# Two of the four weight sums of a 2x2 block product: accumulating transfers from the GpSimd queue in the place of VectorE additions

## The chip, the cores and the metric

The kernel runs on one core of one Trainium2 chip. The metric is the device time of one execution in microseconds (us). The time before is the median of three runs. About 0.3% (some 6 us here) is what a measurement of this kernel can tell from no change.

## The reference

Two transformer blocks run one after the other on 512 tokens of width 1024, all in float32. Only the parts around the change are shown; the attention and recurrence of both blocks are left out.

```python
def hybrid_layer(h, pos, ...):
    ...
    f = rmsnorm(h, norm_ff_w)
    return h + jnp.square(jax.nn.relu(f @ w_ff1)) @ w_ff2      # 1024 -> 4096 -> 1024

def swiglu(u, w_gate, w_up, w_down):
    return (jax.nn.silu(u @ w_gate) * (u @ w_up)) @ w_down     # 1024 -> 2816 -> 1024

def second_block(x, c, ...):
    ...
    u = modulate(rmsnorm_2(h, g_ff1[l]), sh1, sc1)
    h = h + FFN_RES * gt1[:, None, :] * swiglu(u, w1_gate[l], w1_up[l], w1_down[l])
    ...                                                        # attention, mLSTM, merge
    u = modulate(rmsnorm_2(h, g_ff2[l]), sh3, sc3)
    h = h + FFN_RES * gt3[:, None, :] * swiglu(u, w2_gate[l], w2_up[l], w2_down[l])
```

So there are three feed-forward layers: one in the first block (called FF here) and two in the second (FFN1 and FFN2).

## The kernel before

Every float32 product is made from three reduced-precision matmuls. Each operand is split into a rounded high part and the remainder: `split` (L113) lets ScalarE (ACT) write the high part (`wh`, L116) and VectorE (DVE) subtract it from the source (`wl`, L117). TensorE (PE) then multiplies low by high, high by low and high by high.

The first layer of each feed-forward is worked in groups. A group (`w_group`) multiplies a 2x2 block matrix of weights, A11, A21, A22 and A12 (`src[0]` to `src[3]`, each a 128x1024 tile of 512 KB), with a 2x2 block matrix of activations. It does so with seven block products instead of eight, in the manner of Winograd. `w_prod` issues one such product, 24 matmuls of 128x256 (L493). The price of leaving out the eighth product is additions. Those on the weights are four per group, on DVE:

- S = A11 + A21 (L530), into a tile `wS` of its own, of which there is one buffer
- A21 = A21 + A22 (L538), in place
- A11 = A11 + A21 (L539), in place, from the new A21; its split feeds the third product
- A12 = A12 + A11 (L549), in place

There are 8 groups in FF (numbered 0 to 7), 9 in FFN1 (8 to 16) and 9 in FFN2 (17 to 25), 26 in all. In FF the products are finished by multiplications with a row of scales `R` (L305) before they are split as `hh`, `hl`; in FFN1 and FFN2 by a product of two halves (L636).

The order of the products on PE is A11 (first), S, A11', A22, A12, A21', and the last with A12'. The first product of the next group follows the last of this one, so a steady group in the trace begins with 48 matmuls on the bank `x`.

Between the products `fill(j)` puts tiles of the down projection (the second layer), 12 matmuls of 128x512 each (L129 to L131), whose results take turns in two PSUM banks (`mm`). DVE empties such a bank into the residual `res` (L291 in FF, L616 in FFN1 and FFN2). A third tile cannot begin before the first has been emptied. The bank `x` of the products is emptied by L553 (`wq`), before the next product into it.

`w_load` (L473) loads one weight tile, called `raw` whatever its block, through the queue of SyncE (SP). A tile scheduler sets the order in which each engine takes its instructions; each engine then works in this order, and an instruction that waits holds up all that stands behind it on its engine. DVE also does a running product for the conditioning vector (L350).

Of the kernel before, what the change touches and what calls it, by code (L numbers as in the profile page):

```python
# [8 lines left out]
F32 = mybir.dt.float32  # L9
# [5 lines left out]
ALU = mybir.AluOpType  # L15
# [3 lines left out]
P = 128  # L19
T = 512  # L20
# [34 lines left out]
class Kern:  # L55
# [414 lines left out]
        small = self.raws if tag == "raw" else 2  # L470
        return (self.hp if own else self.wp).tile([P, KT, P], dt, name=tag, tag=("s_" if own else "") + tag, bufs=small if own else 3)

    def w_load(self, src, late=2):  # L473

        raw = self.w_tile("raw", F32, late < self.raws - 1).rearrange("p k m -> p (k m)")
        raw = raw[:, :src.shape[-1]]
        self.nc.sync.dma_start(out=raw, in_=src)
        return raw

    def w_split(self, raw, own):  # L480
# [23 lines left out]
    def w_group(self, src, u, tt, ready, evict, fill, early=False):  # L504


        nc, V, act, wk = self.nc, self.nc.vector, self.nc.scalar.activation, self.wk
        blk = lambda h, c: tuple((lambda k, t=t: t[:, 2 * k + h, c * HT:(c + 1) * HT]) for t in u)
        sums = lambda i: tuple((lambda k, t=t: t[:, k, i]) for t in tt)
        X, W, Z = self.bank("x"), self.bank("w"), self.bank("z")  # L510
        tmp = lambda n, tag, pool=wk, b=2: pool.tile([P, T], F32, name=n, tag=tag, bufs=b)
        A11, A21 = self.w_load(src[0], 0), self.w_load(src[1], 1)
        w = self.w_split(A11, True)
        self.w_prod(X, w, *blk(0, 0), first=True)
        p = tmp("wp_", "e1")
        act(out=p, in_=X, func=AF.Copy)
        fill(0)

        def z(A12):
            w = self.w_split(A12, True)  # L520
            self.w_prod(Z, w, *blk(1, 0), first=True)
            V.tensor_tensor(out=p, in0=Z, in1=p, op=ALU.add)

        A22 = A12 = None
        if early:
            A12 = self.w_load(src[3], 0)
            z(A12)
        ready()
        S = self.hp.tile([P, 2 * T], F32, name="wS", tag="wS", bufs=1)
        V.tensor_tensor(out=S, in0=A11, in1=A21, op=ALU.add)  # L530
        w = self.w_split(S, False)
        A22 = self.w_load(src[2])
        A12 = A12 if early else self.w_load(src[3], 0)
        self.w_prod(W, w, *sums(1), first=True)
        q = tmp("wq_", "e2")
        act(out=q, in_=W, func=AF.Copy)
        fill(1)
        V.tensor_tensor(out=A21, in0=A21, in1=A22, op=ALU.add)  # L538
        V.tensor_tensor(out=A11, in0=A11, in1=A21, op=ALU.add)  # L539
        w = self.w_split(A11, True)  # L540
        self.w_prod(X, w, *sums(2))
        un = tmp("wu_", "wu", self.hp, 1)
        act(out=un, in_=X, func=AF.Copy)
        w = self.w_split(A22, False)
        self.w_prod(W, w, *sums(3))
        V.tensor_tensor(out=un, in0=W, in1=un, op=ALU.subtract)
        if not early:
            z(A12)
        V.tensor_tensor(out=A12, in0=A12, in1=A11, op=ALU.add)  # L549
        evict(0, p, un)  # L550
        w = self.w_split(A21, True)
        self.w_prod(X, w, *sums(0))
        V.tensor_tensor(out=q, in0=q, in1=X, op=ALU.subtract)  # L553
        fill(2)
        w = self.w_split(A12, False)
        self.w_prod(X, w, *blk(1, 1))
        evict(1, X, q)
        fill(3)
# [638 lines left out]
    def attention1(self, ap):  # L1197
# [202 lines left out]
        V.tensor_scalar(out=wn05, in0=self.vec("gla_norm_w", 1), scalar1=0.5, scalar2=None, op0=ALU.mult)  # L1400
        go = lambda c, e, S: self.gla_out(c, a2, e, gv, S)
        gate = lambda *cc: self.gla_gate(cc, gv, sr, wn05)
        S = self.gla_meta(ap, a2, dmat, gh, gl, mA, gvm)

# [15 lines left out]

        e, so, S = {}, {}, [S]
        for step in PLAN.split():
# [9 lines left out]
            elif f == "g":  # L1432
                S.append(go(c, e[c], S[-1]))
            elif f == "s":
# [401 lines left out]
```

## Time and profile before

| | before |
|---|---|
| median of 3 runs | 1943.99 us (1940.88 to 1945.86) |
| the profiled execution | 1941.36 us, span 1939.6 us |
| PE busy | 1896.3 us, 98% of the span |
| DVE busy | 1491.1 us, 77% |
| ACT busy | 866.5 us, 45% |
| GpSimd (POOL) busy | 29.9 us, 2% |
| read from HBM | 225.74 MB, 121 GB/s over the span |
| mean granted clock of PE | 0.996 of full speed |

Busy time says how long an engine had work, the span how long the profiled execution took on the chip. The time of the execution has 1.8 us around the span. PE is the engine with nearly no idle time, so only what makes PE wait, or stop waiting, moves the end. The stretches of the trace that the groups fill are about 254 to 590 us (FF), 623 to 960 us (FFN1) and 1560 to 1900 us (FFN2).

### The profile page before, as it was taken

What the parts mean: (1) busy time and instruction counts of PE and PEld (TensorE: products, weight loads), DVE (VectorE), ACT (ScalarE), POOL (GpSimd) and SP (SyncE); (2) the same over time, 40 slices, a digit from 0 to 9 for tenths busy, and PEclk for the clock granted to TensorE, in tenths of its full rate; (3) what the DMA queues carried; (4) which work ended last, traced back from release to release, by engine and by line L of the source; (5) the groups of instructions that cost most, each with busy time, mean ns of one, the idle gap of its engine ahead of it and who ended that gap; (6) DMA issues with size and microseconds to landing.
All of it is one profiled execution on the core that took longest, in us unless ns stands there. A gap on an engine that the chain in (4) does not pass through costs nothing.

```text
span 1939.6 us, 27715 instructions
## 1 busy us (share of the span) xinstructions
PE 1896.3 (98%) x10808; PEld 1583.5 (82%) x10808; DVE 1491.1 (77%) x2592; ACT 866.5 (45%) x1406; POOL 29.9 (2%) x47
## 2 busy tenths in 40 slices
PE   8999999999999899999999999999999999999997
PEld 5775589999988599999887777776678888999996
DVE  6687599888888989888877745677758778877776
ACT  4334465443445544444455444344442245444443
POOL 0000000000000000000000000111100000000000
PEclk9999999999999999999999999999999999999998
DMA  6220145454534154555342231433348732333231
GB/s 197 67 61 12 47 167 167 141 154 147 169 97 146 60 174 146 170 159 179 120 142 87 87 119 58 110 92 96 89 163 298 262 121 78 119 110 109 89 97 55
DMA packets 74333, 240.48 MB, mean 124 GB/s; under 512 B 8997, under 2 KB 12214, under 8 KB 74202
## 3 DMA queue, kind: packets, MB, share of 16 engines
q1 hardware_dynamic: 57274, 189.75, 31.3%
q10 hardware_dynamic: 16928, 48.96, 8.0%
q8 instruction: 85, 1.39, 0.3%
q14 instruction: 46, 0.38, 0.1%
HBM read 225.74 MB, written 8.41 MB: 121 GB/s over the span
## 4 chain that ended last, share of the span: by engine, by line
PE 90%; DVE 7%; ACT 2%; DMA 1%; issue 1%; DVEq 0%; SPq 0%; ACTq 0%
PE x L493 14%; PE mm L131 11%; PE mm L130 11%; PE mm L129 11%; PE mm L123 6%; PE w L493 6%; PE mm L125 6%; PE mm L124 6%; PE z L493 3%; PE po L1652 1%; DVE wl L117 1%; PE sw L1624 1%; PE sc L1041 1%; PE pn L1049 1%; PE po L1178 1%
## 5 line engine op out<-in xcount | busy, mean ns | idle before, releaser
L116 ACT ACTIVATE wh<-raw 128x1024 fp32r<-128x1024 f32 (+1 forms) x371 | 386.3, 1044 | 434.3 <-PE mm L131 128.5
L117 DVE TENSOR_TENSOR wl<-raw,wh 128x1024 fp32r<-128x1024 f32 (+1 forms) x371 | 446.0, 1206 | 117.2 <-ACT wh L116 116.3
L131 PE MATMUL mm<-hh,wh 128*128 128x512 f32 (+1 forms) x640 | 244.7, 382 | 0.0
L130 PE MATMUL mm<-hl,wh 128*128 128x512 f32 (+1 forms) x640 | 244.0, 381 | 0.2 <-DVE hl L117 0.2
L129 PE MATMUL mm<-hh,wl 128*128 128x512 f32 (+1 forms) x640 | 241.6, 378 | 1.4 <-DVE res L688 1.3
L123 PE MATMUL mm<-uh,wl 128*128 128x512 f32 x560 | 224.9, 403 | 2.1 <-ACT uh L116 1.9
L125 PE MATMUL mm<-uh,wh 128*128 128x512 f32 x560 | 223.9, 400 | 0.0
L124 PE MATMUL mm<-ul,wh 128*128 128x512 f32 x560 | 222.9, 398 | 0.3 <-DVE ul L117 0.3
L130 PEld LDWEIGHTS mm<-hl,wh 128*128 128x128 f32 x640 | 120.2, 188 | 23.4 <-DVE hl L117 0.7
L129 PEld LDWEIGHTS mm<-hh,wl 128*128 128x128 f32 x640 | 120.1, 188 | 23.5 <-DVE res L688 1.5
L131 PEld LDWEIGHTS mm<-hh,wh 128*128 128x128 f32 x640 | 120.3, 188 | 21.6
L123 PEld LDWEIGHTS mm<-uh,wl 128*128 128x128 f32 x560 | 105.5, 189 | 35.0 <-issue 6.6
L124 PEld LDWEIGHTS mm<-ul,wh 128*128 128x128 f32 x560 | 105.6, 189 | 23.3 <-issue 1.5
L125 PEld LDWEIGHTS mm<-uh,wh 128*128 128x128 f32 x560 | 105.7, 189 | 23.1 <-issue 2.3
L493 PE MATMUL x<-vh,wl 128*128 128x256 f32 x416 | 116.2, 279 | 0.5 <-DVE wq__6195 L553 0.3
L493 PE MATMUL x<-uh,wl 128*128 128x256 f32 x416 | 115.3, 277 | 1.0 <-DVE wl L117 1.0
L493 PE MATMUL x<-vl,wh 128*128 128x256 f32 x416 | 115.5, 278 | 0.0
L493 PE MATMUL x<-vh,wh 128*128 128x256 f32 x416 | 115.1, 277 | 0.0
L493 PE MATMUL x<-ul,wh 128*128 128x256 f32 x416 | 115.0, 276 | 0.0
L493 PE MATMUL x<-uh,wh 128*128 128x256 f32 x416 | 115.0, 276 | 0.0
L350 DVE CUSTOM_DVE_ANT_0 adaw<-adaw,cb,c_vecs 128x1024 f32<-128x1024 f32 x72 | 91.4, 1278 | 15.0 <-DMA adaw<-in_w_ada 15.0
L616 DVE SCALAR_TENSOR_TENSOR res<-mm,gt,res 128x512 f32<-128x512 f32 x88 | 65.5, 747 | 23.3 <-PE mm L131 23.1
(960 smaller groups left out, 4250.3 us busy)
## 6 DMA issues: line engine op xcount, KB each, us to landing
adaw<-in_w_ada ACTq DMA_DIRECT2D x72, 512.0 KB
raw<-in_wgw SPq DMA_DIRECT2D x72, 512.0 KB
raw<-in_wdw SPq DMA_DIRECT2D x40, 512.0 KB
raw<-in_w_ffw SPq DMA_DIRECT2D x32, 512.0 KB
raw<-in_w_ffd SPq DMA_DIRECT2D x32, 512.0 KB
raw<-in_wgu SPq DMA_DIRECT2D x24, 512.0 KB
raw<-in_w_g SPq DMA_DIRECT2D x20, 512.0 KB
raw<-in_w_out SPq DMA_DIRECT2D x16, 512.0 KB
```

Source lines behind the costliest of these rows:

```text
L116: nc.scalar.activation(out=h, in_=src, func=AF.Copy)
L117: nc.vector.tensor_tensor(out=l, in0=src, in1=h.bitcast(F32), op=ALU.subtract)
L123: mm(ps, lhsT=wl[:, k], rhs=xh[:, k], start=(k == order[0]), stop=False)
L124: mm(ps, lhsT=wh[:, k], rhs=xl[:, k], start=False, stop=False)
L125: mm(ps, lhsT=wh[:, k], rhs=xh[:, k], start=False, stop=(k == order[-1]))
L129: mm(ps, lhsT=al, rhs=bh, start=(k == 0), stop=False)
L130: mm(ps, lhsT=ah, rhs=bl, start=False, stop=False)
L131: mm(ps, lhsT=ah, rhs=bh, start=False, stop=(k == last))
L350: ins = nc.vector.tensor_tensor_reduce(out=w, in0=w, in1=self.cb, scale=0.5, scalar=self.vec("b_ada_2", 72)[:, i:i + 1], op0=ALU.mult, op1 ...
L493: mm(o, lhsT=l[:, a, k], rhs=r(k), start=(first and a == 0 and k == 0 and j == 0), stop=(k == 3 and j == 2), skip_group_check=True)
L616: V.scalar_tensor_tensor(out=res[:, m], in0=ps, scalar=gt[:, m:m + 1], in1=res[:, m], op0=ALU.mult, op1=ALU.add)
L1041: mm(pk[:, :n], lhsT=k[:, kt, j * P:(j + 1) * P], rhs=q[:, kt, j * P:], start=(kt == 0), stop=(kt == 1))
```

## The change

S is no longer added on DVE: a second load through SP puts A11 into the tile `wS`, and a transfer from POOL's queue adds A21 to it on its way in. The load of A21 is likewise followed by a transfer from POOL's queue that adds A22 to it. A22 is still loaded by itself for its own product. L530 and L538 are gone, and the numbers of later lines rise: A11 = A11 + A21 is L543, A12 = A12 + A11 is L553, the emptying of `x` L557, that of `mm` in FFN1 and FFN2 L620, the products of two halves L640.

```diff
-    def w_load(self, src, late=2):
+    def w_load(self, src, late=2, plus=None):
 
         raw = self.w_tile("raw", F32, late < self.raws - 1).rearrange("p k m -> p (k m)")
         raw = raw[:, :src.shape[-1]]
         self.nc.sync.dma_start(out=raw, in_=src)
+        if plus is not None:
+
+            self.nc.gpsimd.dma_start(out=raw, in_=plus, accum_op=ALU.add)
         return raw
...
-        A11, A21 = self.w_load(src[0], 0), self.w_load(src[1], 1)
+        A11 = self.w_load(src[0], 0)
+        S = self.hp.tile([P, 2 * T], F32, name="wS", tag="wS", bufs=1)
+        nc.sync.dma_start(out=S, in_=src[0])
+        nc.gpsimd.dma_start(out=S, in_=src[1], accum_op=ALU.add)
+        A21 = self.w_load(src[1], 1, src[2])
...
         ready()
-        S = self.hp.tile([P, 2 * T], F32, name="wS", tag="wS", bufs=1)
-        V.tensor_tensor(out=S, in0=A11, in1=A21, op=ALU.add)
         w = self.w_split(S, False)
...
-        V.tensor_tensor(out=A21, in0=A21, in1=A22, op=ALU.add)
         V.tensor_tensor(out=A11, in0=A11, in1=A21, op=ALU.add)
```

The scheduler moves what remains. In the first place, group 2 of FF on DVE, the rows before are these; `raw_3047` is A11, `raw_3049` A21, `raw_3090` A22, and `mm_2920`, `mm_2940` and `mm_2954` are three tiles of the down projection one after the other:

```order
L553 TENSOR_TENSOR wq__2733<-wq__2733,x_2659 128x512 [waits PE_49]
L350 ISA adaw_3081,mods_2368<-adaw_3081,cb_2369,c_vecs_72 128x1024 [waits DMAHW6_49]
L350 ISA mods_2368 128x1
L117 TENSOR_TENSOR hl_2658<-wp__2694,hh_2657 128x2x256 [waits DVE_49,Activation_49]
L291 TENSOR_TENSOR res_2083<-mm_2920,res_2083 128x512 [waits PE_49]
L305 SCALAR_TENSOR_TENSOR wq__2733<-wq__2733,R_2398 128x512 [waits DVE_49]
L117 TENSOR_TENSOR wl_3011<-raw_3008,wh_3010 128x1024 [waits DMAHW3_49,Activation_49]
L291 TENSOR_TENSOR res_2083<-mm_2940,res_2083 128x512 [waits PE_49]
L530 TENSOR_TENSOR wS_3084<-raw_3047,raw_3049 128x1024 [waits DMAHW0_49]
L117 TENSOR_TENSOR hl_2658<-wq__2733,hh_2657 128x2x256 [waits DVE_49,Activation_49]
L538 TENSOR_TENSOR raw_3049<-raw_3049,raw_3090 128x1024 [waits DMAHW4_49,DVE_49]
L291 TENSOR_TENSOR res_2083<-mm_2954,res_2083 128x512 [waits PE_49]
```

Now the same place reads as follows; `raw_3049` is A11 here, `raw_3054` the A21 that two transfers fill, `mm_2922` the first of the three tiles:

```order
L350 ISA adaw_3087,mods_2368<-adaw_3087,cb_2369,c_vecs_72 128x1024 [waits DMAHW2_49]
L350 ISA mods_2368 128x1
L117 TENSOR_TENSOR hl_2659<-wp__2699,hh_2658 128x2x256 [waits DVE_49,Activation_49]
L117 TENSOR_TENSOR hl_2659<-wu__2824,hh_2658 128x2x256
L557 TENSOR_TENSOR wq__2736<-wq__2736,x_2660 128x512 [waits PE_49]
L543 TENSOR_TENSOR raw_3049<-raw_3049,raw_3054 128x1024 [waits DMASW5_49,DVE_49]
L291 TENSOR_TENSOR res_2083<-mm_2922,res_2083 128x512 [waits PE_49]
L305 SCALAR_TENSOR_TENSOR wq__2736<-wq__2736,R_2398 128x512 [waits DVE_49]
L117 TENSOR_TENSOR wl_3013<-raw_3010,wh_3012 128x1024 [waits DMAHW6_49,Activation_49]
L291 TENSOR_TENSOR res_2083<-mm_2942,res_2083 128x512 [waits PE_49]
```

A11 = A11 + A21 has moved up, from behind the fourth emptying of a bank to a place ahead of the first; its wait on `DMASW5` is the wait for POOL's accumulating transfer.

In the second place, a steady group of FFN2 on DVE, the rows before are these; `raw_16238` is A11, `raw_16240` A21 and `x_15935` the bank that the group's seventh product needs emptied:

```order
L538 TENSOR_TENSOR raw_16240<-raw_16240,raw_16278 128x1024 [waits DMAHW0_49,DVE_49]
L117 TENSOR_TENSOR wl_16275<-wS_16272,wh_16274 128x1024 [waits Activation_49]
L522 TENSOR_TENSOR wp__15970<-z_15937,wp__15970 128x512 [waits PE_49]
L117 TENSOR_TENSOR wl_16243<-raw_16238,wh_16242 128x1024 [waits Activation_49]
L636 TENSOR_TENSOR wp__15970<-wp__15970,wu__16072 128x512 [waits Activation_49]
L553 TENSOR_TENSOR wq__16006<-wq__16006,x_15935 128x512 [waits PE_49]
L539 TENSOR_TENSOR raw_16238<-raw_16238,raw_16240 128x1024 [waits DVE_49]
L117 TENSOR_TENSOR hl_15934<-wp__15970,hh_15933 128x2x256 [waits Activation_49]
L616 SCALAR_TENSOR_TENSOR res2_14027<-mm_16172,gt2_14559,res2_14027 128x512 [waits PE_49]
```

Now the same place reads as follows, with `raw_16260` for A11 and `raw_16265` for A21:

```order
L117 TENSOR_TENSOR wl_16299<-wS_16262,wh_16298 128x1024 [waits DMASW4_49,Activation_49]
L529 TENSOR_TENSOR wp__15995<-z_15958,wp__15995 128x512 [waits PE_49]
L117 TENSOR_TENSOR wl_16269<-raw_16260,wh_16268 128x1024 [waits DMAHW1_49,Activation_49]
L640 TENSOR_TENSOR wp__15995<-wp__15995,wu__16094 128x512 [waits Activation_49]
L543 TENSOR_TENSOR raw_16260<-raw_16260,raw_16265 128x1024 [waits DMASW5_49,DVE_49]
L117 TENSOR_TENSOR hl_15955<-wp__15995,hh_15954 128x2x256 [waits Activation_49]
L557 TENSOR_TENSOR wq__16029<-wq__16029,x_15956 128x512 [waits PE_49]
L117 TENSOR_TENSOR wl_16368<-raw_16260,wh_16367 128x1024 [waits Activation_49]
L620 SCALAR_TENSOR_TENSOR res2_14044<-mm_16194,gt2_14576,res2_14044 128x512 [waits PE_49]
```

The addition, with its wait for POOL's transfer, stands ahead of the emptying of `x` instead of behind it.

In the third place, the head of FFN1 on DVE, the addition and the split behind it now stand in the middle of a row of tiny instructions that works out a reciprocal square root for the layer's activations. Before, the same root (L186 and what follows) held none of them; L530 and the split of A11 stood in the root ahead of it:

```order
L186 TENSOR_SCALAR rs_v_5643<-s2_5634 128x4 [waits DVE_49]
L187 TENSOR_SCALAR rs_t_5644<-rs_v_5643 128x4 [waits DVE_49]
L188 TENSOR_SCALAR r2_5642<-rs_t_5644 128x4 [waits DVE_49]
L190 TENSOR_TENSOR rs_t_5644<-r2_5642 128x4 [waits DVE_49]
L191 SCALAR_TENSOR_TENSOR rs_t_5644<-rs_t_5644,rs_v_5643 128x4 [waits DVE_49]
```

Now the root begins as follows, with `raw_6135` for A11 and `raw_6140` for A21:

```order
L186 TENSOR_SCALAR rs_v_5651<-s2_5642 128x4 [waits DVE_49]
L543 TENSOR_TENSOR raw_6135<-raw_6135,raw_6140 128x1024 [waits DMASW1_49]
L187 TENSOR_SCALAR rs_t_5652<-rs_v_5651 128x4 [waits DVE_49]
L117 TENSOR_TENSOR wl_5873<-raw_5871,wh_5872 128x1024 [waits DMAHW6_49,Activation_49]
L188 TENSOR_SCALAR r2_5650<-rs_t_5652 128x4 [waits DVE_49]
L117 TENSOR_TENSOR wl_6212<-raw_6135,wh_6211 128x1024 [waits Activation_49]
L190 TENSOR_TENSOR rs_t_5652<-r2_5650 128x4 [waits DVE_49]
```

L543 and the split `wl_6212` stood some 80 instructions later before.

## Rows read from the trace of the kernel before

**Rows 1.** The page, busy time, share of the span and instructions of each engine

```profile
PE 1896.3 (98%) x10808; PEld 1583.5 (82%) x10808; DVE 1491.1 (77%) x2592; ACT 866.5 (45%) x1406; POOL 29.9 (2%) x47
```

**Rows 2.** Windows: stretch, length; busy PE, PEld, DVE, ACT, POOL; clock, DMA share, GB/s

```profile
254.00:320.00 66.00, 64.72 (x400) 57.05 (x399) 64.26 (x96) 37.06 (x51) 0.00 (x0) 1.00 0.42 133
320.00:590.00 270.00, 270.00 (x1739) 244.08 (x1738) 224.62 (x301) 116.47 (x145) 0.00 (x0) 1.00 0.48 145
615.00:620.00 5.00, 5.00 (x25) 4.02 (x23) 4.67 (x7) 4.21 (x7) 0.00 (x0) 1.00 1.01 362
650.00:670.00 20.00, 13.10 (x47) 9.33 (x48) 19.81 (x34) 11.05 (x18) 0.00 (x0) 0.91 0.05 14
700.00:710.00 10.00, 9.54 (x80) 9.11 (x79) 10.00 (x13) 5.39 (x9) 0.00 (x0) 1.00 0.49 151
720.00:960.00 240.00, 240.00 (x1726) 221.72 (x1725) 208.30 (x271) 106.80 (x132) 0.00 (x0) 1.00 0.50 158
1650.00:1660.00 10.00, 8.81 (x76) 8.51 (x75) 8.28 (x10) 4.23 (x6) 0.00 (x0) 1.00 0.34 111
1680.00:1900.00 220.00, 220.00 (x1582) 205.45 (x1581) 164.82 (x178) 97.61 (x119) 0.00 (x0) 1.00 0.32 97
```

**Rows 3.** Line L530: its instructions (shortest, median, longest ns), then its engine's wait

```profile
L530 DVE TENSOR_TENSOR wS<-raw x26: 1211/1222/1227, 260.8 to 1858.5; 128x1024 f32<-128x1024 f32 x26
...
  DMA raw<-in_wgw: 8.8, 11
```

**Rows 4.** Line L538: its instructions

```profile
L538 DVE TENSOR_TENSOR raw<-raw x26: 1215/1216/1226, 262.8 to 1860.3; 128x1024 f32<-128x1024 f32 x26
```

**Rows 5.** Chain that ended last, at two group starts: start us, length us, what

```profile
693.63 4.73 DMA raw<-in_wgw
...
1649.53 3.89 DMA raw<-in_wgw
...
1653.52 1.24 DVE wS L530
```

**Rows 6.** SP's queue: issue of A21's load, groups 2, 3, FFN1, FFN2

```profile
324.13 0.33 SPq L477 DMA_DIRECT2D raw<-in_w_ffw  x1
...
363.36 0.33 SPq L477 DMA_DIRECT2D raw<-in_w_ffw  x1
...
780.63 0.33 SPq L477 DMA_DIRECT2D raw<-in_wgw  x1
...
1764.67 0.33 SPq L477 DMA_DIRECT2D raw<-in_wgw  x1
```

**Rows 7.** DVE in order of time: start, length, line, operation, out<-in [idle before]

```profile
331.11 0.68 DVE L291 TENSOR_TENSOR res<-mm,res 128x512 f32<-128x512 f32 x1
...
371.03 0.68 DVE L553 TENSOR_TENSOR wq__3118<-wq__3118,x 128x512 f32<-128x512 f32 x1
...
623.33 1.22 DVE L530 TENSOR_TENSOR wS<-raw 128x1024 f32<-128x1024 f32 x1
...
628.60 0.17 DVE L186 TENSOR_SCALAR rs_v<-s 128x4 f32<-128x4 f32 x1
...
788.72 0.68 DVE L553 TENSOR_TENSOR wq__7082<-wq__7082,x 128x512 f32<-128x512 f32 x1
...
1768.44 1.23 DVE L530 TENSOR_TENSOR wS<-raw 128x1024 f32<-128x1024 f32 x1 [0.64 <-DMA raw<-in_wgw]
...
1774.79 0.68 DVE L553 TENSOR_TENSOR wq__16006<-wq__16006,x 128x512 f32<-128x512 f32 x1
```

**Rows 8.** Chain on PE: first matmul of two third tiles, seventh products of two groups

```profile
333.11 0.23 PE mm L129
...
374.14 0.23 PE mm L129
...
793.86 2.72 PE x L493 x24
...
1778.62 5.44 PE x L493 x48
```

## The prediction

> **What bounds the kernel now.** I read the page's busy times first. PE works 1896.3 us, 98% of the span, DVE 77%, POOL 2% [rows 1]. PE is the engine with hardly any idle time, so a DVE addition is worth something only where PE waits for DVE. The windows show where that is, and they were read next. In the long stretches of steady groups PE is busy for the whole of the stretch: 270.00 of 270 us in FF, 240.00 of 240 in FFN1, 220.00 of 220 in FFN2, while DVE has 224.62, 208.30 and 164.82 us of work there [rows 2]. Nothing can be gained in these 730 us. Idle time of PE near the groups stands in four places: 1.28 us at the start of FF (254 to 320, where DVE has 64.26 of 66), 6.90 us in the head of FFN1 (650 to 670, where DVE has 19.81 of 20), 0.46 us at 700 to 710 and 1.19 us at 1650 to 1660 [rows 2]. Their sum, 9.8 us, is all that the change could ever touch.
>
> Then I read the two lines that go. L530 has 26 instructions of 1.222 us, L538 26 of 1.216 us [rows 3, 4]: 63.4 us of DVE work leave. L530 stood behind a load 11 times, 8.8 us in all [rows 3]. The chain of waits runs through such a load at two group starts, from 693.63 and from 1649.53, and through L530 itself at 1653.52 [rows 5].
>
> **The change part by part.** I work each part as a difference and add it to the median of the runs, 1943.99; the profiled execution (1941.36, of which 1939.6 is span) lies 2.6 us below that median, and the durations are its own.
>
> *What goes.* In steady groups the 63.4 us are hidden behind a PE that is never idle: 0. At the start of group 18 the chain runs load 3.89, then L530 1.24, to the next product [rows 5]; S now comes ready-made, and the idle 1.19 us go. At 700 to 710 DVE is full for all of 10 us with L530 in it [rows 2]; the 0.46 us go. Together -1.7.
>
> *What is added.* 26 more loads through SP and 52 accumulating transfers through POOL, 512 KB each. That is 41 MB (78 x 524,288 bytes), of which 27 MB are accumulated. The DMA share in the steady stretches is 0.32 to 0.50 [rows 2], so there is room for it. S is read early (its load and transfer have most of a group's 30 us), and its split waits for nothing that is late: 0.
>
> The term that decides is A21. Before, A11 = A11 + A21 (L539) stood behind two DVE additions and needed only plain loads. Now, as L543, it waits for a chain: load of A21, then POOL wakes, then the accumulating transfer. While it waits, all of DVE stands, since the queue is in order. Let X be the time from A21's landing to the release of L543. No POOL transfer stands in this trace, so X is bounded by rows. A plain load takes 3.77 us from its issue (1764.67) to the DVE instruction that waited for it (1768.44) [rows 6, 7]. The accumulation reads two streams and writes one, where a plain load reads one and writes one. It should not be quicker than one plain load, 3.8 us, and hardly slower than two of the longest such piece in the chain, 2 x 4.73 = 9.5 us [rows 5]. I take three streams for two, 1.5 x 3.77 = 5.7 us, which is nearer to the row of one load.
>
> By the Trainium skill (DMA: Bandwidth & Descriptors, "Anatomy of one DMA — SWDGE (gpsimd) path") a transfer from GpSimd takes about 2.0 us and its bytes at 436 GB/s, 3.2 us for 512 KB. With each byte read twice, 4.4 us by my estimate, the sum below would be about 1.5 us smaller. No run here shows it yet.
>
> How late may the transfer be? From the issue of A21's load to the latest start of L543 that costs PE nothing there is a slack; the load takes 3.77 of it, and the rest is the X that is free.
> - Group 2 of FF: L543 now stands ahead of the emptying of a `mm` bank that began at 331.11, and the third tile needs this bank at 333.11 [rows 7, 8]. The addition (1.22) and the emptying (0.68) must begin by 331.21. The load is issued at 324.13 [rows 6]. Slack 7.08, free X 3.3; at 5.7 it costs +2.4.
> - Group 3: third tile at 374.14 [rows 8], so a start by 372.24; issue 363.36 [rows 6]. Slack 8.88, free X 5.1; +0.6. (The place on DVE is behind the row at 371.03 [rows 7], so DVE itself begins to stand at X = 4.6.) In groups 4 to 7 the load goes out earlier: 0, unless X passes 9.5.
> - FFN1, groups 9 to 16: L543 now stands ahead of the split of `hl` and the emptying of `x`, which was at 788.72, and the seventh product needs `x` at 793.86 [rows 7, 8]. Addition, split and emptying take 1.22 + 0.68 + 0.68 = 2.58, so a start by 791.28; issue 780.63 [rows 6]. Slack 10.65, free X 6.9: 0 at 5.7. One group was taken for all eight.
> - FFN2, groups 18 to 25: in the same way 1778.62 - 2.58 - 1764.67 = 11.37 [rows 6, 8], free X 7.6: 0. The emptying stood at 1774.79 [rows 7], and DVE has a quarter of its time free there.
>
> *The head of FFN1.* L543 and the split behind it moved into the reciprocal root at 628.60, ahead of the stretch in which DVE is the bound [rows 2, 7]. They bring 2 x 1.22 us there, and L530 at 623.33 takes 1.22 away. A21 had landed by 623.33 at the latest, since L530 read it then, so L543 has 5.4 us (623.33 to 628.77) for X: at 5.7 a stand of 0.3. The cover is thin, since the DMA engines are full at 615 to 620 (share 1.01, 362 GB/s) [rows 2]. Between nothing and 1.2 + (9.5 - 5.4) = 5.3 I take +1.5.
>
> *The start of FF.* DVE loses 2.4 us of additions in groups 0 and 1, where PE idles 1.28 us; but A21's load of group 0 is now behind S's on SP, and L543 has moved up. Between -1.3 and +3.8 (one load's time) I take 0.
>
> Sum: -1.7 + 2.4 + 0.6 + 1.5 = +2.8, so 1946.8, say 1947.
>
> **Rivals.** *The accumulation is slow, and DVE stands in every group* (this ends slower). The price is X less the free X, times the groups. At X = 7.5: 4.2 + 2.4 + 8 x 0.6 + 0 + (1.2 + 2.1) - 1.7 = +13, 1957. At 9.5: 6.2 + 4.4 + 8 x 2.6 + 8 x 1.9 + 5.3 - 1.7 = +50, 1994. It decides from X = 6.9 on, only 1.2 us above the value I took. For it speaks that POOL's share of the work (waking, preparing a transfer) is in none of my rows; against it, that the DMA engines are half empty in these stretches.
>
> The Trainium skill (SBUF — State Buffer, "SBUF: two separate sides") warns that descriptors of a GpSimd transfer cannot be written while DVE runs an instruction in a two-port mode. With DVE at 83% of FF's stretch [rows 2] such a lock-out would lengthen X. The page says that it is a copy within SBUF that takes this mode, and the DVE rows here are mostly two-input additions; so it adds little to this rival's chance.
>
> *The accumulation is as quick as a load.* X = 3.8 leaves group 2 at +0.5, the head near 0: -1.2 in all, or -2.5 with the start of FF gained, so 1941.5 to 1943. The early place of the loads speaks for it, two reads in place of one against it.
>
> *The DVE relief reaches PE* (faster). If the stands are all hidden, and the head gains from DVE's lighter load too, half its 6.9 us with the 1.28 + 0.46 + 1.19 of the other places make -6.4, 1937.6. Against it: the order of the head brings work to DVE ahead of its bound stretch, not away.
>
> **How the numbers follow.** A difference below 0.3%, 5.8 us, is what a measurement cannot tell from none: 1938.2 to 1949.8. Chances: the forecast (X between 4.5 and 6.9, 1941 to 1952) 0.43; slow accumulation (1952 to 1994) 0.32; quick accumulation 0.18; relief 0.07. Of the forecast 0.37 lies within 0.3% and 0.06 above; of the quick case 0.16 within and 0.02 below. So faster 0.07 + 0.02 = 0.09, same 0.37 + 0.16 = 0.53, slower 0.06 + 0.32 = 0.38. The range reaches down to 1940 and, into the slow case, up to 1980.
>
> **What would show it.** On the line of L543, the idle time of DVE ahead of it that ended with the accumulating transfer: some 4 us in all if I am right (groups 2 and 3 and the head), 30 us or more if the accumulation is slow, and then PE waits for DVE or ACT in every group of FFN1 and FFN2. The transfer's own landing time gives X. At 1650 to 1660 and 700 to 710 PE should be without idle time. If X is under 6.9 and PE still loses several us per group, something other than the wait at L543 is at work, and the argument is wrong.

## The result: 3.4% slower

The changed kernel took 2008.04 us (median of 4 runs, 2003.37 to 2020.44) against 1942.88 us, a ratio of 1.0344 over all runs (the two medians alone give 1.0335) with a 95% interval of 1.0294 to 1.0394. That is 65 us more, outside the range that was given. The profiled execution is the longest of the four (2020.44 us, span 2018.7), so its parts add up to more than the 65 us; they are compared with the profiled execution of before.

Busy times on the page of the changed kernel, and the queue that is new (packets, MB, share):

```profile
PE 1926.1 (95%) x10808; PEld 1605.1 (80%) x10808; DVE 1439.4 (71%) x2540; ACT 863.4 (43%) x1406; POOL 75.3 (4%) x99
...
q0 software_dynamic: 7488, 27.27, 7.9%
```

Against [rows 1] DVE is busy 51.7 us less: L530 and L538 are gone (63.4 us when each instruction is counted by itself; neighbours overlap in the record), but its waiting has grown. PE has the same 10808 matmuls and is busy 29.8 us longer, and its idle time has grown from 43.3 us (1939.6 - 1896.3) to 92.6 us. So the span's 79.1 us are 49.3 us of waiting and 29.8 us of longer busy time, most of it matmuls at a lower granted clock (mean 0.982 against 0.996).

The line of the addition that waits for POOL's transfer (as in [rows 3]: its instructions, its engine's waits, who waited for it):

```profile
L543 DVE TENSOR_TENSOR raw<-raw x26: 1210/1226/1228, 263.5 to 1944.8; 128x1024 f32<-128x1024 f32 x26
...
  DMA raw<-in_wgw: 92.4, 18
  DMA raw<-in_w_ffw: 11.3, 4
...
  ACT wh L116: 122.2, 24
```

DVE stood 104 us ahead of L543, in 22 of 26 groups; ACT stood 122 us behind it. The transfers themselves, on the page's list of issues (KB each, median us from issue to landing):

```profile
wS<-in_wgw POOLq DMA_DIRECT2D x18, 512.0 KB, 6.8
raw<-in_wgw POOLq DMA_DIRECT2D x18, 512.0 KB, 8.2
...
wS<-in_w_ffw POOLq DMA_DIRECT2D x8, 512.0 KB, 6.8
raw<-in_w_ffw POOLq DMA_DIRECT2D x8, 512.0 KB, 5.5
```

One steady group of FFN1 (number 12) in the chain of waits, start, length, what:

```profile
850.50 4.88 DMA raw<-in_wgw
...
855.41 0.04 POOLq L480
855.45 0.60 issue
856.05 7.55 DMA raw<-in_wgw
...
863.70 1.23 DVE raw L543
864.92 0.60 DVE hl L117
865.53 0.60 DVE wq__7430 L557
```

and, behind it, PE in order of time:

```profile
866.18 0.39 PE L496 MATMUL x<-vh,wl 128*128 128x256 f32 x1 [2.44 <-DVE wq__7430 L557]
```

(The lag of group 12 comes from the addition of the next group, which DVE reaches before it empties group 12's `x`.) This is the chain that the slow rival named: load of A21, POOL's wake-up, accumulating transfer, L543, the split of `hl`, the emptying of `x`, and only then the seventh product on PE. From the load's issue to L543 it is 863.70 - 850.50 = 13.2 us. The slack worked out from before was 10.65 us; the difference, 2.55 us, is what PE waited (2.44).

The waiting costs twice. Windows of the changed kernel around the same wait in group 11, and last the one behind the 2.44 us of group 12 (columns as in [rows 2]; the clock is the third number from the right):

```profile
829.00:831.00 2.00, 1.05 (x7) 1.05 (x8) 2.00 (x3) 1.82 (x2) 0.00 (x0) 0.90 0.00 0
831.00:833.00 2.00, 2.00 (x11) 2.00 (x11) 2.00 (x4) 0.00 (x0) 0.00 (x0) 0.50 0.00 0
833.00:835.00 2.00, 2.00 (x16) 1.83 (x15) 1.79 (x3) 0.38 (x1) 0.00 (x0) 0.74 0.24 35
835.00:837.00 2.00, 2.00 (x20) 1.85 (x18) 1.49 (x2) 2.00 (x5) 0.00 (x0) 1.00 0.88 309
...
866.50:868.50 2.00, 2.00 (x19) 2.00 (x18) 2.00 (x3) 0.55 (x1) 0.00 (x0) 1.00 0.00 0
```

After the gap in group 11, in a stretch that was full before, the granted clock is at 0.50 of full speed, the lower of its two levels (1.2 GHz), and comes back some us later: 11 matmuls in 2 us, then 16, then 20. The same followed six of the seven waits of 2.3 to 3.7 us at the emptying of `x` in FFN1; after the 2.44 us of group 12 the clock stayed at 1.00. In the steady stretches of before it was 1.00 throughout [rows 2]. By stretch, FFN1 and FFN2 now read:

```profile
740.00:990.00 250.00, 229.71 (x1591) 211.93 (x1590) 177.12 (x229) 98.89 (x124) 11.34 (x13) 0.96 0.65 181
1700.00:1950.00 250.00, 235.03 (x1665) 218.53 (x1665) 156.69 (x168) 101.07 (x124) 13.22 (x16) 0.98 0.55 145
```

### The profile page after: what moved, and what is told of

It reads as the page before. It is cut to its first block, busy times and chain, and to the rows that moved or that the text cites. A ratio compares the mean times of both kernels' runs of the same rounds, so it can differ in the third digit from the quotient of the medians.

```text
span 2018.7 us, 27903 instructions
## 1 busy us (share of the span) xinstructions
PE 1926.1 (95%) x10808; PEld 1605.1 (80%) x10808; DVE 1439.4 (71%) x2540; ACT 863.4 (43%) x1406; POOL 75.3 (4%) x99
## 4 chain that ended last, share of the span: by engine, by line
PE 67%; DMA 14%; DVE 13%; issue 3%; ACT 3%; SPq 0%; DVEq 0%; ACTq 0%; POOLq 0%
PE x L496 10%; DMA raw<-in_wgw 9%; PE mm L130 8%; PE mm L131 8%; PE mm L129 8%; PE mm L123 5%; PE mm L125 5%; PE mm L124 5%; PE w L496 4%; DVE wl L117 3%; DMA adaw<-in_w_ada 2%; DMA raw<-in_w_ffw 2%; PE z L496 1%; DVE raw L543 1%; PE po L1656 1%
## 5 line engine op out<-in xcount | busy, mean ns | idle before, releaser
L496 PE MATMUL x<-vh,wl 128*128 128x256 f32 x416 | 122.4, 294 | 22.5 <-DVE wq__7762 L557 3.7
L496 PE MATMUL x<-uh,wl 128*128 128x256 f32 x416 | 118.6, 285 | 15.6 <-DVE wq__14893 L557 6.3
L125 PEld LDWEIGHTS mm<-uh,wh 128*128 128x128 f32 x560 | 105.5, 188 | 22.9 <-issue 2.3
L496 PE MATMUL x<-vl,wh 128*128 128x256 f32 x416 | 120.2, 289 | 0.5 <-DVE vl L117 0.5
L496 PE MATMUL x<-vh,wh 128*128 128x256 f32 x416 | 120.0, 289 | 0.0
L496 PE MATMUL x<-ul,wh 128*128 128x256 f32 x416 | 117.1, 282 | 0.0
L496 PE MATMUL x<-uh,wh 128*128 128x256 f32 x416 | 117.0, 281 | 0.0
L543 DVE TENSOR_TENSOR raw<-raw 128x1024 f32<-128x1024 f32 x26 | 31.8, 1224 | 103.7 <-DMA raw<-in_wgw 92.4
L496 PEld LDWEIGHTS x<-vh,wl 128*128 128x128 f32 x416 | 83.3, 200 | 26.5 <-DVE wq__7762 L557 3.8
```

The costliest lines, as they stand in the source:

```text
L125: mm(ps, lhsT=wh[:, k], rhs=xh[:, k], start=False, stop=(k == order[-1]))
L496: mm(o, lhsT=l[:, a, k], rhs=r(k), start=(first and a == 0 and k == 0 and j == 0), stop=(k == 3 and j == 2), skip_group_check=True)
```

## The experiments

A table shows where each kernel loses its time. The emptying of `x` (L553 before, L557 after) happens once a group; its start in the profiled execution, less the start before, is the lag at that group (us; groups 0, 8 and 17 are the first of FF, FFN1 and FFN2). The lags are those of one execution each, the last column compares medians, so the two can differ.

| kernel | 0 | 2 | 3 | 7 | 8 | 9 | 10 | 15 | 17 | 18 | 24 | median - before |
|---|---|---|---|---|---|---|---|---|---|---|---|---|
| the change | 4.9 | 6.4 | 10.2 | 9.9 | 17.1 | 29.7 | 35.8 | 58.3 | 64.5 | 69.2 | 81.6 | +65.2 |
| 1: S only | -0.2 | -0.2 | -0.2 | -0.5 | 2.3 | 3.0 | 3.2 | 5.2 | 6.1 | 5.0 | 5.2 | +6.2 |
| 2: A21 only | 1.1 | 2.7 | 8.9 | 7.6 | 14.4 | 20.6 | 27.8 | 51.8 | 50.3 | 53.8 | 60.8 | +57.2 |
| 3: order edge | 6.2 | 6.0 | 5.7 | 5.7 | 11.7 | 12.5 | 14.4 | 14.0 | 21.1 | 19.8 | 20.4 | +23.4 |
| 4: both into S | 4.2 | 4.2 | 8.0 | 12.2 | 14.9 | 16.2 | 15.9 | 25.7 | 33.4 | 35.0 | 35.6 | +31.3 |
| 5: plain transfers | 3.2 | 3.3 | 3.1 | 3.0 | 5.3 | 8.9 | 13.0 | 20.3 | 22.0 | 24.6 | 23.6 | +23.9 |
| 6: edge, starts on DVE | -1.2 | -1.1 | -1.1 | -1.4 | -1.2 | -2.6 | -1.3 | -1.6 | -1.8 | -3.9 | -3.2 | -1.8 |
| 7: S only, less the starts | 1.9 | 1.8 | 1.8 | 1.5 | 2.3 | 2.6 | 2.9 | 4.3 | 7.7 | 6.7 | 6.8 | +3.7 |

The theory: L543 waits in DVE's queue for a transfer that lands late, and holds up all that is behind it. The rival: the traffic of the transfers slows the other loads, whoever waits.

**1. S only.** The addition for A21 returns to DVE.

```diff
-        A21 = self.w_load(src[1], 1, src[2])
+        A21 = self.w_load(src[1], 1)
...
+        V.tensor_tensor(out=A21, in0=A21, in1=A22, op=ALU.add)
         V.tensor_tensor(out=A11, in0=A11, in1=A21, op=ALU.add)
```

> One half of the change: S by a load and an accumulating transfer, A21 + A22 on DVE as before (26 of the 52 transfers). Theory (DVE stands at A11 = A11 + A21, L543, for A21's late accumulating transfer, with all that is queued behind it, and PE's clock drops in the gaps): S is read half a group after its transfer, nothing stands, so the time is near before, 1938 to 1947 us. Rival (the traffic of the accumulating transfers and GpSimd's part slow other loads, whoever waits): half of the 65 us, about 1975.

Measured: 1948.61 us, ratio 1.0035 (1.0021 to 1.0049). Half of the transfers cost 6 us, not half of 65; but it is 2 us above what the theory expected, and no gain.

**2. A21 only.** S is a plain load of A21's block, to which DVE adds A11.

```diff
-        nc.sync.dma_start(out=S, in_=src[0])
-        nc.gpsimd.dma_start(out=S, in_=src[1], accum_op=ALU.add)
+        nc.sync.dma_start(out=S, in_=src[1])
...
+        V.tensor_tensor(out=S, in0=S, in1=A11, op=ALU.add)
         w = self.w_split(S, False)
```

> The other half: A21 + A22 by the accumulating transfer (26 of 52), S by a plain load of A21's block into wS and an addition of A11 on DVE. Theory: the wait at A11 = A11 + A21 stays, so most of the loss stays, 1985 to 2010 us; the transfer may land sooner than the 8 us of the changed kernel, since no second accumulating transfer is in flight beside it, which would take some us off. Rival (traffic): half the loss, about 1975.

Measured: 1999.68 us, ratio 1.0291 (1.0276 to 1.0306). The A21 transfer alone carries 57 of the 65 us. It landed in 7.3 us (median of FFN1 and FFN2) against 8.2, as was thought possible without the other transfer beside it.

**3. The order edge.** All 52 transfers stay; L543 may only be placed behind the last emptying of a down-projection bank (`anchor`, the last L291 or L616/L620 that was written ahead of the group).

```diff
+        anchor, self.last_res = getattr(self, 'last_res', None), None
         A11 = self.w_load(src[0], 0)
...
-        V.tensor_tensor(out=A11, in0=A11, in1=A21, op=ALU.add)
+        add = V.tensor_tensor(out=A11, in0=A11, in1=A21, op=ALU.add)
+        if anchor is not None:
+            self.after(anchor, add)
```

> The changed kernel, all 52 transfers, with one edge of order: A11 = A11 + A21 may not be placed ahead of the down projection's bank emptyings of the group before (about where it stood before the change). Theory: DVE reaches it some 5 to 8 us later, when the transfer has landed, so the waits in FFN1's and FFN2's steady groups and in FFN1's head go: 1945 to 1960 us (the first groups of FF, FFN1 and FFN2 keep theirs). Rival (traffic): nothing changes, about 2008. A third view (the wait moves to the next reader, PE's third product): 1975 to 2000.

Measured: 1965.84 us, ratio 1.0118 (1.0103 to 1.0133). 42 of the 65 us are gone with the same transfers, in the same numbers, from the same queue. The addition's line in this kernel:

```profile
L548 DVE TENSOR_TENSOR raw<-raw x26: 1212/1218/1227, 264.6 to 1891.2; 128x1024 f32<-128x1024 f32 x26
...
  DMA raw<-in_wgw: 8.7, 2
  DMA raw<-in_w_ffw: 7.4, 1
```

22 waits have become 3, 104 us have become 16. A21's transfers land no sooner (8.1 us, median); DVE only comes to the addition later. The lag is flat through all steady groups, and what is left stands at the starts, some 6 us at each of groups 0, 8 and 17. The waits that remain are those of groups 0 (7.4 us), 9 (2.7) and 18 (6.0, ahead of the emptying of group 17). At group 8 L548 waits for nothing; there DVE stood for a load for the conditioning vector, and PE then 4.7 us for a split behind it:

```profile
700.23 1.28 DVE L350 CUSTOM_DVE_ANT_0 adaw<-adaw,cb,c_vecs 128x1024 f32<-128x1024 f32 x1 [5.42 <-DMA adaw<-in_w_ada]
```

That load took 7.60 us. The time was 6 us above the upper end of the expectation, since the starts cost more than had been allowed for. For the steady groups this decides against the rival, as the traffic is unchanged; for the start of FFN1 it does not.

**4. The traffic without the late wait.** Both transfers of a group go into S's tile, one behind the other; A21 + A22 is made on DVE. S then holds another sum.

```diff
         nc.gpsimd.dma_start(out=S, in_=src[1], accum_op=ALU.add)
+        nc.gpsimd.dma_start(out=S, in_=src[2], accum_op=ALU.add)
-        A21 = self.w_load(src[1], 1, src[2])
+        A21 = self.w_load(src[1], 1)
```

> As many accumulating transfers as the changed kernel (52, 512 KB each), but both of a group go into S's tile, one behind the other, and A21 + A22 is done on DVE as before; so S holds A11 + A21 + A22, which is another sum. Theory: all the traffic, no late wait, so near the first half alone, 1938 to 1950 us. Rival (traffic): about 2008.

Measured: 1973.78 us, ratio 1.0170 (1.0129 to 1.0211), between the two expectations. It separates less than it should: with two transfers in a row S itself came late (its split stood for it twice, 10.2 us on ACT and 9.5 us on DVE), and A21 + A22 on DVE stood 22.9 us for plain loads that now landed later (11.5 us in the first run, which has half the transfers). Its line:

```profile
L544 DVE TENSOR_TENSOR raw<-raw x26: 1212/1224/1227, 266.6 to 1893.6; 128x1024 f32<-128x1024 f32 x26
...
  DMA raw<-in_wgw: 22.9, 14
```

So transfers do delay loads beside them, and the rival is not empty; but where nobody is close behind the transfer, as in the steady groups of the third run, it costs nothing.

**5. Plain transfers.** The order on PE, DVE, POOL and SP is the changed kernel's, row for row; the 52 transfers overwrite their tile in place of adding to it, so S and A21 hold other numbers.

```diff
-            self.nc.gpsimd.dma_start(out=raw, in_=plus, accum_op=ALU.add)
+            self.nc.gpsimd.dma_start(out=raw, in_=plus)
...
-        nc.gpsimd.dma_start(out=S, in_=src[1], accum_op=ALU.add)
+        nc.gpsimd.dma_start(out=S, in_=src[1])
```

> The changed kernel with the same order on every engine and the same 52 transfers from GpSimd's queue, but plain ones: they overwrite the tile in place of adding to it (so two of the weights of each block product are other numbers). It tells how much of X is the accumulation and how much the path through GpSimd. If the accumulation itself is slow (three streams in place of two, as I had argued): the transfer lands in about two thirds of the 8.2 us, some 5.5 us, X falls by nearly 3 us, and with 17 late steady groups the time falls by 30 to 45 us, to 1963 to 1978. If the path through GpSimd or the traffic is what is slow: landing near 8 us, time near 2008.

Measured: 1966.89 us, ratio 1.0137 (1.0120 to 1.0154). The issues, and the addition's line:

```profile
wS<-in_wgw POOLq DMA_DIRECT2D x18, 512.0 KB, 4.7
raw<-in_wgw POOLq DMA_DIRECT2D x18, 512.0 KB, 5.4
```

```profile
L543 DVE TENSOR_TENSOR raw<-raw x26: 1217/1226/1228, 261.5 to 1886.7; 128x1024 f32<-128x1024 f32 x26
...
  DMA raw<-in_wgw: 44.9, 18
  DMA raw<-in_w_ffw: 5.4, 3
```

A transfer that is 2.8 us shorter gives 41 us back, as expected. The accumulating transfer is 8.2 / 5.4 = 1.52 times as long as the plain one (1.34 for A21 in FF, 1.45 and 1.48 for S). The plain one from POOL's queue is itself late: L543 still stands in 21 groups. From the load's issue to L543 it is 10.7 to 12.6 us in FFN1's groups 10 to 16, where the slack is 10.65, and the lag grows by 11.4 us from group 9 to 15; in FFN2's groups 19 to 25 it is 9.1 to 11.5 us against 11.37, and the lag does not grow.

**6. The edge, and the starts on DVE.** The third kernel, but groups 0, 8, 9, 17 and 18 make S and A21 on DVE as before (`dve`); 42 transfers are left.

```diff
-        A21 = self.w_load(src[1], 1, src[2])
+        A21 = self.w_load(src[1], 1, None if dve else src[2])
...
+        if dve:
+            V.tensor_tensor(out=A21, in0=A21, in1=A22, op=ALU.add)
```

> The kernel with the order edge, but groups 0, 8, 9, 17 and 18 (the first of each layer, and the second of FFN1 and FFN2) make their sums on DVE as before; 42 accumulating transfers are left, all in steady groups. The third run left 6 us at each layer's start and little between. Theory: those starts go and the rest is hidden, 1942 to 1948 us, not faster than before since PE has no idle time in the steady groups. Rival (the remaining transfers' traffic costs by itself): 1952 to 1962.

Measured: 1941.21 us, ratio 0.9995 (0.9986 to 1.0004): no difference from before. The whole loss is gone, with four fifths of the transfers still there, and 42 DVE additions fewer buy nothing.

**7. S only, less the starts.** The first kernel, but groups 0, 8 and 17 add S on DVE.

```diff
-        nc.sync.dma_start(out=S, in_=src[0])
-        nc.gpsimd.dma_start(out=S, in_=src[1], accum_op=ALU.add)
+        if not dve:
+            nc.sync.dma_start(out=S, in_=src[0])
+            nc.gpsimd.dma_start(out=S, in_=src[1], accum_op=ALU.add)
```

> S by load and accumulating transfer in all groups but 0, 8 and 17, A21 + A22 on DVE everywhere. The first run (S alone, in all 26 groups) was 6 us slower than before, and its lag grew at the starts of FFN1 and FFN2 and by 2 us in groups 14 and 15. Theory: without the starts 1941 to 1945 us, the same as before or 1 to 2 us faster, as S is ready early in groups 9 and 18. Rival (the cost is spread over all groups as traffic): 1947 to 1949.

Measured: 1946.69 us, ratio 1.0019 (1.0010 to 1.0028). This was expected at 1941 to 1945 and fell outside. It is just below the rival's 1947, but in the table the lag hardly grows through the steady groups, where a cost that is spread over all groups would have it grow. Of the 6.3 us that its profiled execution is longer, PE's idle time is 2.4 us (1945.9 - 1900.2 against 43.3) and 3.9 us are longer busy time. The lag is 1.9 us already at group 0, which adds S on DVE: the clock was at 0.50 from 177 to 184 us, long before the first transfer at 279. Near group 9 PE waited 1.5 us for a split; S's own split on DVE stood for nothing there, and the chain runs through a plain load (5.01 us, 4.73 before). So S's transfer is not seen to be late, and what makes up the 3.7 us is open, as it is for the 6.2 us of the first run.

## Why the prediction was wrong

The step that failed is the forecast's price for the chain of A21: X was taken as 5.7 us, within a free X of 6.9 in FFN1, and measured 8.3, so DVE stood at L543 in nearly every group. Two more terms were too small: the starts, put at +1.5 us and measured at 35.6, and PE's waits, priced without the clock.

*What bounds the kernel* held. PE is the bound, and taking additions off DVE in full stretches gave nothing: sixth run, -1.8 us, which its interval does not tell from none.

*The term that decides* was named rightly and mis-sized: X was taken as 5.7 us and is 863.70 - 855.38 = 8.3 us in the group shown, 6.1 to 9.8 us in FFN1 from group 9 on and 8.0 to 10.5 in FFN2 from group 18 on. The factor was near: three streams for two, 1.5, against 1.34 to 1.52 measured between the accumulating and the plain transfer; that the third stream is the cause is not shown. What it was applied to was wrong. I took a plain load from SP's queue, 3.77 us, as the base; a plain transfer from POOL's queue lands 5.4 us after its issue, and POOL needs 0.64 us to issue it once the load has landed (855.41 to 856.05).

Beside that, the 3.77 us are a row of FFN2, and I used them for A21's load in FFN1 too. There the load was longer before the change already, 5.4 us in the group shown here and 5.3 and 4.9 in the two after it:

```profile
844.78 2.41 SPq L477 DMA_DIRECT2D raw<-in_wgw  x2
...
850.14 1.23 DVE L530 TENSOR_TENSOR wS<-raw 128x1024 f32<-128x1024 f32 x1 [1.05 <-DMA raw<-in_wgw]
```

So the X that was free in FFN1 was 5.3 to 5.8 us and not 6.9, none to spare even for 5.7. In the changed kernel the load took 4.88 us in the group shown.

By the Trainium skill (DMA: Bandwidth & Descriptors, "Anatomy of one DMA — SWDGE (gpsimd) path") a transfer of 512 KB takes 3.2 us, and with its bytes counted twice 4.4 us by my estimate; the measured medians are 5.4 and 8.2 us, the shortest 3.8 and 5.3. The measurement decides. (With 4.4 us the forecast's sum falls by 1.9 us, 1.3 in group 2 and 0.6 in group 3, and not by about 1.5.)

*The slacks* held, but for FF's group 2. FFN1: 13.2 us against 10.65 foretold a wait of 2.55 us, and 2.44 was seen. Worked out in the same way, PE's waits at the emptying of `x` come out within 0.16 us in groups 9 to 14 and 18 to 24 (not in 15 and 17). In FF's group 3, 10.71 us against 8.88 foretold 1.83, and 1.80 was seen; in group 2, 9.84 against 7.08 foretold 2.76, and 0.83 was seen, as the load went out about 2 us earlier against PE than before. That the two groups cost 4.0 us together (lag 6.2 at group 1 to 10.2 at group 3), near the 3.0 of the forecast, is luck: 0.2 came in group 2 and 3.8 in group 3, where 2.4 and 0.6 had been expected, with an X of 6.2 and 7.2 us and a clock of 0.64 from 384 to 388 us. FFN2, with its larger slack, lost less per group than FFN1: 12.4 us from group 18 to 24 against 28.6 from 9 to 15.

*The sum* left out the clock. Every PE wait was priced at its own length, and 29.8 of the 79.1 us are longer busy time, most of it matmuls at the lower granted clock. From the seventh product of group 9 to that of group 15 PE needs 217.53 us where it needed 190.34, of which it is busy 199.81 and 190.34 (before, then now, columns as in [rows 2]):

```profile
731.65:921.99 190.34, 190.34 (x1377) 176.02 (x1376) 167.23 (x213) 87.09 (x107) 0.00 (x0) 1.00 0.53 166
...
759.04:976.57 217.53, 199.81 (x1377) 184.16 (x1377) 153.62 (x200) 84.75 (x107) 9.59 (x11) 0.96 0.65 184
```

The 27.2 us are 17.7 us of waiting, 17.4 of it at the emptying of `x` in groups 10 to 15, and 9.5 us of longer busy time. The two longest and the shortest of these waits at `x`, in the changed kernel's list of PE's waits (us in all, times, longest; L496 is the products' matmul):

```profile
PE x L496 <- DVE wq__7762 L557: 3.7, 1, 3.7
PE x L496 <- DVE wq__8460 L557: 3.5, 1, 3.5
...
PE x L496 <- DVE wq__6754 L557: 2.3, 1, 2.3
```

*The starts* failed worst. I took 0 for FF's and +1.5 for FFN1's, and counted -1.7 as won at groups 9 and 18. Growth of the lag: +4.9 at group 0, +7.2 at group 8, +12.6 at group 9, +6.2 at group 17 (from group 15), +4.7 at group 18, 35.6 us in all. The bounds were wrong in their parts, not in the place. In FFN1's head DVE stood 6.45 us in the reciprocal root, the new place of L543:

```profile
642.57 1.23 DVE L543 TENSOR_TENSOR raw<-raw 128x1024 f32<-128x1024 f32 x1 [6.45 <-DMA raw<-in_wgw]
```

There A21's load took 6.11 us and its transfer 10.44 us, with S's transfer and other loads in flight beside it. In group 9 L543 stood 5.23 us, until 728.99, for a transfer of 9.07 us, and PE waited 2.4 us for `hh` and 1.1 us for `hl` of the group before; then the next L543 stood 5.30 us, until 756.56, ahead of the emptying of `x`. I had looked only at what S's early arrival would save there. The third run, with the edge, takes back the growth at groups 9 and 18 (+0.8 and -1.3 there), and the sixth, in which these five groups keep their DVE additions, the some 6 us that were left at each of 0, 8 and 17.

*The rivals.* The slow accumulation, given 0.32, is what happened: its chain and its place, and the sign that was named for it (104 us at L543, where 30 or more had been set). Its size was short: by its own sum X = 8.3 gives +27 us, and 8.7, the median in FFN1 and FFN2, +35. The rest of the 65 us are FFN1's longer loads, the clock and the starts, so a right X alone would not have given the time. Its decision point, X = 6.9, lay between the plain transfer's 5.4 + 0.6 and the accumulating one's 8.3; that even plain transfers cost 24 us agrees with the 5.3 to 5.8 us that were free in FFN1. Nothing was seen of the lock-out of GpSimd by DVE that the Trainium skill (SBUF — State Buffer, "SBUF: two separate sides") warns of: POOL's instruction took 862 to 901 ns wherever it stood in FFN1 and FFN2, with 1007 once in FF.

What stays open: the 6.2 us of the first run and the 3.7 us of the seventh, what made the load ahead of group 8 late in the third, and how much of an accumulating transfer's length is its second read and how much the transfers beside it (A21's landed in 7.3 us in the second run, without S's, against 8.2).

## What to carry to other kernels

Work that moves from an engine to a transfer moves its wait too: the first reader on an in-order queue now stands for load, wake-up and transfer one after the other, and all behind it stands with it. So work out from the trace when that reader comes up and when the data can be there, and if the second is later, pin the reader further back before anything else; here one edge of order gave back 42 of 65 us. A bound engine that was never idle can also lose clock when it begins to wait, so a wait on it can cost more than its length (here 1.5 times over a steady stretch, 27.2 us of lag to 17.7 of waits). And take the length of a transfer from the stretch in which it is to run: the same load took 3.77 us in FFN2 and about 5 in FFN1.

## What the runs showed of the hardware

- An accumulating transfer of 512 KB from GpSimd's queue landed 5.3 to 10.4 us after its issue (median 7.9 over all of A21's), a plain one in the same place 3.8 to 7.6 (median 5.0). POOL itself was busy 0.87 us with issuing the first kind and 0.53 us with the second.
- After six of the seven PE waits of 2.3 to 3.7 us at the emptying of `x` in FFN1, in a stretch that had been full, the granted clock stood at 0.50 of full speed for some us; after one of 2.44 us it stayed at 1.00.
